# Five raw weight buffers in place of three, out of shared SBUF space, and the first half's row transposes four to five matmuls later at a stage's end

## The chip, the cores and the metric

The kernel runs on one core of a Trainium2 chip. The metric is the device time of one execution in microseconds (us); of several executions the median is given.

## What is computed

A decoder trunk of four layers on one sequence of 256 rows with 1024 features. Each layer is a SwiGLU feed-forward half step, a token mixer, and a second feed-forward half step, each between two RMS norms with a gain:

```python
def swiglu_ffn(x, w_gate_up, w_down):
    gate, up = jnp.split(x @ w_gate_up, 2, axis=-1)
    return (jax.nn.silu(gate) * up) @ w_down
...
x = x + 0.5 * rms_norm(swiglu_ffn(rms_norm(x, g0), ...), g1)     # the sandwich, in short
x = x + rms_norm(mixer(rms_norm(x, g2)), g3)
```

The hidden width is 2816. The mixer of layers 0 and 3 is a gated MLP over chunks of rows (mixer a), that of layer 1 a dilated window attention with rotary tables (mixer b), that of layer 2 a forgetting attention (mixer c). Each mixer also attends to 256 memory rows. All is in 32-bit floating point.

## The kernel before

**Stages and halves.** The 256 rows are two halves of 128, t = 0 and t = 1, held in `x[0]` and `x[1]`. The program is twelve stages: FFN(l,0), mixer, FFN(l,1) for each layer l. A stage begins with transposed inputs `xth` and `xtl` and ends with a boundary: ScalarE squares a half's result and VectorE multiplies it with the gain `gpost` (`L373`, `L374`), GpSimd makes the inverse root, VectorE adds to `x` (`L378`), ScalarE squares `x` (`L381`), GpSimd makes the second inverse root (`L348`, `L349`), VectorE writes the normed rows with the gain `gpre` (`L385`), TensorE transposes the rows (`L399`), and ScalarE and VectorE split the result into `xth` and `xtl` (`L309`, `L310`).

**Three products for one.** A 32-bit matmul is made of three faster ones: a value is split into a rounded part hi and a rest lo, and hi·hi, lo·hi and hi·lo are added up (`L334`, `L335`, `L336`; in the down projection all three are `L684`). So each unit of weights, 128x1024 numbers or 512 KB, goes this way: a transfer by SP's queue into one of RAW buffers `raw` (`L240`), ScalarE's copy into `hi` (`L309`), VectorE's subtraction into `lo` (`L310`), and then the matmuls. The pair `hi`, `lo` is a ring of ten. A `raw` buffer is free again when its `lo` is made; a ring place when the last matmul that reads it is through. The order of units is a plan; `pump` makes as many as the ring has room for, and `slot`, called after each unit's matmuls, also issues one background step (`self.bg`).

**The FFN.** The hidden columns are six sets. Sets 0, 1, 3 and 5 are plain. Sets 2 and 4 form their 2x2 blocks from seven products instead of eight (function `seven`, matmuls on `L615`); their weights are loaded into `quad` buffers (eight transfers) and VectorE adds some of them up first (`L277`). Between the products VectorE and ScalarE take results out: `L635` (function `c11`, from PSUM into `snap`), `L658` and `L659` (function `c12`). A finished set `T` is transposed on TensorE at `L557` (`turn_set`) and split into `hh` and `hl` (for the last set `eh` and `el`), the left sides of the down projection. The down projection has 22 units; the last eight are held at the end: first all eight for t = 0, then the chain of the boundary for t = 0 is issued (`turn(0)`), then the eight for t = 1, which are 48 matmuls of 128x512, then `turn(1)`. The transposes of t = 0 (`trans(0)`) are issued right after `turn(0)`, ahead of the eight units of t = 1; a scheduler that reorders by readiness then places them. The transposes of t = 1 are issued inside the next stage's first set.

**The mixers** end in the same way: `out_first` makes the out projection of t = 0, `out_rest` issues `trans(0)` and the out projection of t = 1 (`L944`; eight units, in mixer b four), then the second boundary chain.

**The scheduler.** The program is written as if in sequence; a scheduler fixes each engine's order from readiness and priority, and the engines run their lists in that order, waiting on semaphores. SP's list holds nearly all transfers.

**SBUF.** Pools hand out buffers by tag. Before the change RAW is 3; the ScalarE squares are dumped into a tag `junk`; memory rows and their chunks have the tags `gpost` and `memraw`; the two gains of a boundary have the tags `gpost` and `gpre` for the whole program and are loaded by the background step `gains` at the start of each FFN (in FFN(0,0) after set 2); the sums of the seven products have the tags `sh` and `sl`.

Of the kernel before, what the change touches and what calls it, by code (L numbers as in the profile page):

```python
# [10 lines left out]
F32 = mybir.dt.float32  # L11
# [19 lines left out]
LN_EPS = 1e-5  # L31
BIG = 1e30
RING = 10
RAW = 3
HELD = 8
GRP = 4

# [166 lines left out]
class Trunk:  # L204
# [143 lines left out]
        g.tensor_tensor(out=out, in0=ss, in1=eps_tile, op=ALU.add)  # L348
        g.tensor_tensor(out=out, in0=out, in1=self.neghalf, op=ALU.pow)  # L349

    def gain(self, l, n, tag):
        t = self.main.tile([P, D], F32, tag=tag, name=tag)
        self.nc.sync.dma_start(out=t, in_=self.io["norm_g"][l, n].partition_broadcast(P))
        return t

    def ln_stages(self, st, t, ps, post_scale, post_eps, gpost, gpre):
        nc = self.nc
        if "rows" not in st:
            st["rows"] = None
        junk = lambda: self.main.tile([P, D], BF16, tag="junk", name="junk")  # L360
        ss = self.small.tile([P, 1], F32, tag="ss", name="ss", bufs=8)
        r = self.small.tile([P, 1], F32, tag="r", name="r", bufs=8)
        ss2 = self.small.tile([P, 1], F32, tag="ss2", name="ss2", bufs=8)
        r2 = self.small.tile([P, 1], F32, tag="r2", name="r2")
        x = self.x[t]

        def rows():
            if st["rows"] is None:
                st["rows"] = self.main.tile([P, 2, D], F32, tag="rows", name="rows")
            return st["rows"][:, t, :]  # L370

        def s1():
            nc.scalar.activation(out=junk(), in_=ps, func=AF.Square, scale=post_scale, accum_out=ss)  # L373
            nc.vector.tensor_tensor(out=rows(), in0=ps, in1=gpost, op=ALU.mult)  # L374
            self.rsqrt(r, ss, post_eps)

        def s2():
            nc.vector.scalar_tensor_tensor(out=x, in0=rows(), scalar=r, in1=x, op0=ALU.mult, op1=ALU.add)  # L378

        def s3():  # L380
            nc.scalar.activation(out=junk(), in_=x, func=AF.Square, scale=1 / 32, accum_out=ss2)  # L381
            self.rsqrt(r2, ss2, self.eps1)

        def s4():
            nc.vector.scalar_tensor_tensor(out=rows(), in0=x, scalar=r2, in1=gpre, op0=ALU.mult, op1=ALU.mult)  # L385

        out = []
        if ps is not None:
            out += [s1, s2]
        if gpre is not None:  # L390
            out += [s3, s4]
        return out
# [36 lines left out]
    def setup(self):  # L429
        nc, io, c = self.nc, self.io, self.const  # L430
        self.x = [c.tile([P, D], F32, name=f"x{t}") for t in range(2)]
        self.ident = c.tile([P, P], F32, name="ident")
        nc.sync.dma_start(out=self.x[0], in_=io["x"][:P, :])
        self.gpre = self.gain(0, 0, "gpre")
# [12 lines left out]
        turn = self.boundary(None, None, self.gpre)  # L447
        turn(0)
        self.trans(0, keep=self.keep)
        turn(1)  # L450
        self.pump(most=RING)

    def setup2(self):
        nc, io, c = self.nc, self.io, self.const
        self.tri1 = c.tile([P, SEQ], F32, name="tri1")
        self.R = c.tile([P, SEQ], F32, name="R")

        def loads():
            nc.sync.dma_start(out=self.tri1, in_=io["tri1"])
            nc.sync.dma_start(out=self.mg, in_=io["mem_g"])  # L460

        def squares(t):
            m = self.main.tile([P, D], F32, tag="gpost", name="memrow")
            nc.sync.dma_start(out=m, in_=io["mem"][t * P:(t + 1) * P, :])
            ss = self.small.tile([P, 1], F32, tag="ss", name="ss", bufs=8)
            nc.scalar.activation(out=self.main.tile([P, D], BF16, tag="junk", name="junk"), in_=m, func=AF.Square,
                                 scale=1 / 32, accum_out=ss)
            self.rsqrt(self.r_mem[:, t:t + 1], ss, self.eps1)

        def inverse():  # L470
            ps = self.rot()
            for t in range(2):
                d = self.main.tile([P, SEQ], F32, tag="memraw", name="memf", bufs=2)
# [55 lines left out]
    def ffn(self, l, f, post_next, pre_next, last=False):  # L529
        nc, tc = self.nc, self.tc  # L530
        with tc.tile_pool(name=f"ffn{l}{f}", bufs=1, reuse_waits="tile") as fp:
# [61 lines left out]
            def sums():  # L593
                x11, x12, x21, x22 = (self.xf[t, h] for t in range(2) for h in range(2))
                tt = nc.vector.tensor_tensor
                out = []
                for dst, a, b, op in ((x22, x21, x22, ALU.subtract), (x21, x11, x21, ALU.subtract),
                                      (x11, x22, x11, ALU.subtract), (x12, x12, x11, ALU.add)):
                    tt(out=dst, in0=a, in1=b, op=op)
                    y = tuple(fp.tile([P, 4, P], F32R, tag=n, name=n, bufs=4) for n in ("sh", "sl"))  # L600
                    self.split(*(v.rearrange("p a b -> p (a b)") for v in y), dst)
                    out.append(y)
                S1, S3, S2, S4 = out
                a11 = tuple(v[:, 0:4, 0:P] for v in xt)
# [60 lines left out]
            gn = {"pre": None}  # L665

            def gains():
                gn["post"] = self.gain(l, post_next[0], "gpost")
                if pre_next:
                    gn["pre"] = self.gain(*pre_next, "gpre")  # L670

            if (l, f) != (0, 0):
                self.bg.append(gains)
            ys = [self.acc() for _ in range(2)]

            def hT(j, t):
                return tuple(h[:, j % 4, t * P:(t + 1) * P] for h in hs[j // 4])

            def down(j, t, w):
                a = hT(j, t)  # L680
                mm = nc.tensor.matmul
                for x, y in ((a[0], w[0]), (a[0], w[1]), (a[1], w[0])):
                    for n in range(2):
                        mm(ys[t][:, n * 512:(n + 1) * 512], x, y[:, 0, n * 512:(n + 1) * 512],  # L684
                           start=(j == 0 and x is a[0] and y is w[0]),
                           stop=(j == NF - 1 and x is a[1]))
# [14 lines left out]
            for s in range(1, SETS):  # L701
# [2 lines left out]
                    self.new_quad(fp, l, f, s + 1)  # L704
                if s in SEVEN:
                    seven(s)
                    if s == min(SEVEN) and (l, f) == (0, 0):
                        self.bg.extend(self.setup2() + [gains])
                    if s == min(SEVEN) and (l, f) == (0, 1):
                        self.bg.extend(self.rope_tables(fp))  # L710
                    if s == max(SEVEN) and f == 0:
# [22 lines left out]
                    turned(SETS - 1)  # L734
            turn = self.boundary(ys, (gn["post"], 1 / 16, self.eps16), gn["pre"])
            turn(0)
            if not last:
                self.trans(0, keep=self.keep if f else None)
            for j in range(nd, NF):
                down(j, 1, held[j - nd])  # L740
                self.slot(1)
            turn(1)
        if last:
# [1 line left out]
                nc.sync.dma_start(out=self.io["out"][t * P:(t + 1) * P, :], in_=self.x[t])  # L745

    def mem_chunk(self, k):
        m = self.main.tile([P, SEQ], F32, tag="memraw", name="memraw", bufs=2)
        self.nc.sync.dma_start(out=m, in_=self.io["mem_t"][k * P:(k + 1) * P, :])
        return m  # L750

# [180 lines left out]

        return o, [lambda j=j: self.out_step(l, o, 0, j) for j in range(n)], chain

    def out_step(self, l, o, t, j):
        if j == 0:
            o["y"].append(self.acc())
        if t == 0:
# [1 line left out]
        w = o["w"][j]  # L940
        a = tuple(v[:, j, t * P:(t + 1) * P] for v in o["yt"])
        for x, y in ((a[0], w[0]), (a[0], w[1]), (a[1], w[0])):
            for h in range(2):
                self.nc.tensor.matmul(o["y"][t][:, h * 512:(h + 1) * 512], x, y[:, 0, h * 512:(h + 1) * 512],  # L944
                                      start=(j == 0 and x is a[0] and y is w[0]),
# [1 line left out]
        self.slot(t)  # L947

    def out_rest(self, l, o):
        self.trans(0, keep=self.keep)  # L950
        for j in range(o["n"]):
            self.out_step(l, o, 1, j)
        o["turn"](1)

    def mixer(self, l, j):
# [4 lines left out]
            getattr(self, "mix_" + kind)(mp, l, j, self.xt)  # L960

    def gains(self, l):
        return self.gain(l, 3, "gpost"), self.gain(l, 4, "gpre")

    def mix_a(self, mp, l, j, xt):
        nc, io = self.nc, self.io
# [362 lines left out]
```

## Time and profile before

| | |
|---|---|
| median of 3 executions | 1900.68 us (1900.43 to 1908.29) |
| the profiled execution | 1902.04 us |
| its span (first to last instruction) | 1900.2 us |
| granted TensorE clock, mean over the span | 0.999 of full speed |
| busy: PE, PEld | 1858.8, 1550.4 us (98%, 82%) |
| busy: DVE, ACT, POOL | 1514.9, 1085.9, 59.8 us (80%, 57%, 3%) |
| moved by the DMA queues | 362.65 MB, mean 191 GB/s |

PE is TensorE's matmuls, PEld its weight loads, DVE VectorE, ACT ScalarE, POOL GpSimd, SP the engine that issues the transfers, SPq its queue. 1.84 us of the profiled execution lie outside its span. Each row of the chain and of the waits names an engine, an output tile and a line of the kernel, and what it waited for.

### The profile page before, as it was taken

To read this page: it belongs to the slowest core of one execution; us is meant where nothing else is said; L and a number is where in the kernel's file an instruction comes from. 1 tells how busy PE (TensorE), PEld (TensorE's weight loads), DVE (VectorE), ACT (ScalarE), POOL (GpSimd) and SP (SyncE) were. 2 spreads that over 40 slices of the span, in tenths; PEclk is the share of its full clock that TensorE was granted. 3 is DMA by queue.
4 is the path that set the end of the run, shared out by engine and by line. 5 is a ranking of instruction groups with operands and counts; after the bars stand their busy time and mean duration, and the time that the engine had idled before them with its cause. 6 is when DMAs were issued, how large, how long until landed. Compare 5 with 4: busy or idle time off the path is not lost.

```text
span 1900.2 us, 25015 instructions
## 1 busy us (share of the span) xinstructions
PE 1858.8 (98%) x9406; PEld 1550.4 (82%) x9406; DVE 1514.9 (80%) x1828; ACT 1085.9 (57%) x1469; POOL 59.8 (3%) x115
## 2 busy tenths in 40 slices
PE   7999999999999999999999999999999999999998
PEld 5888888787878897888888889888888878988886
DVE  6987888896879768889697966878877886878894
ACT  5655656564656545655565656555556555656562
POOL 0000100000000000000000000000000000100000
PEclk9999999999999999999999999999999999999999
DMA  8646747545663663754566357275476535747632
GB/s 295 235 167 200 233 156 266 205 140 176 233 222 115 199 203 111 266 198 145 180 231 233 112 185 238 102 246 184 151 229 227 189 127 183 243 156 244 220 105 86
DMA packets 103865, 362.65 MB, mean 191 GB/s; under 512 B 12084, under 2 KB 16576, under 8 KB 103616
## 3 DMA queue, kind: packets, MB, share of 16 engines
q1 hardware_dynamic: 103568, 359.47, 56.5%
q8 instruction: 74, 1.21, 0.3%
q0 software_dynamic: 176, 1.59, 0.2%
q14 instruction: 47, 0.39, 0.1%
HBM read 359.95 MB, written 1.06 MB: 190 GB/s over the span
## 4 chain that ended last, share of the span: by engine, by line
PE 60%; DVE 17%; DMA 12%; ACT 5%; issue 4%; POOL 1%; ACTq 0%; SPq 0%; DVEq 0%
PE acc L684 15%; DMA raw<-in_w 12%; PE rot L615 9%; PE rot L334 9%; PE rot L336 9%; PE rot L335 9%; DVE lo L310 9%; ACT hi L309 4%; DVE quad L277 3%; PE acc L944 3%; PE rot L557 1%; PE rot L399 1%; PE rot L848 1%; DVE x L378 1%; PE rot L880 1%
## 5 line engine op out<-in xcount | busy, mean ns | idle before, releaser
L310 DVE TENSOR_TENSOR lo<-raw,hi 128x1024 fp32r<-128x1024 f32 (+1 forms) x515 | 624.4, 1219 | 216.9 <-ACT hi L309 207.5
L309 ACT ACTIVATE hi<-raw 128x1024 fp32r<-128x1024 f32 (+1 forms) x515 | 542.1, 1055 | 397.0 <-DMA raw<-in_w 259.0
L334 PE MATMUL rot<-hi,xth 128*128 128x512 f32 (+3 forms) x1072 | 414.9, 387 | 2.5 <-ACT hi L309 1.6
L336 PE MATMUL rot<-hi,xtl 128*128 128x512 f32 (+3 forms) x1072 | 411.6, 384 | 1.2 <-DVE xtl L310 1.1
L335 PE MATMUL rot<-lo,xth 128*128 128x512 f32 (+3 forms) x1072 | 411.6, 384 | 0.0
L309 ACT ACTIVATE hi<-quad 128x1024 fp32r<-128x1024 f32 x224 | 232.7, 1056 | 156.5 <-DVE quad L277 83.4
L310 DVE TENSOR_TENSOR lo<-quad,hi 128x1024 fp32r<-128x1024 f32 x224 | 269.4, 1220 | 7.2 <-ACT hi L309 6.2
L334 PEld LDWEIGHTS rot<-hi,xth 128*128 128x128 f32 x1072 | 202.1, 189 | 41.4 <-ACT hi L309 2.1
L336 PEld LDWEIGHTS rot<-hi,xtl 128*128 128x128 f32 x1072 | 201.9, 188 | 41.3 <-DVE xtl L310 2.3
L335 PEld LDWEIGHTS rot<-lo,xth 128*128 128x128 f32 x1072 | 202.1, 189 | 38.2
L684 PE MATMUL acc<-lo,hh 128*128 128x512 f32 x640 | 198.9, 390 | 0.0
L684 PE MATMUL acc<-hi,hh 128*128 128x512 f32 x640 | 198.0, 390 | 0.0
L684 PE MATMUL acc<-hi,hl 128*128 128x512 f32 x640 | 197.2, 389 | 0.0
L277 DVE TENSOR_TENSOR quad<-quad 128x1024 f32<-128x1024 f32 x128 | 154.2, 1220 | 0.9
L684 PEld LDWEIGHTS acc<-hi,hl 128*128 128x128 f32 x640 | 120.1, 188 | 25.0 <-DVE hl L310 0.2
L684 PEld LDWEIGHTS acc<-lo,hh 128*128 128x128 f32 x640 | 120.2, 188 | 24.8
L684 PEld LDWEIGHTS acc<-hi,hh 128*128 128x128 f32 x640 | 119.5, 188 | 24.3
L615 PE MATMUL rot<-hi,sh 128*128 128x512 f32 x256 | 103.0, 402 | 6.8 <-DVE snap L635 6.8
L615 PE MATMUL rot<-lo,sh 128*128 128x512 f32 x256 | 100.0, 391 | 0.0
L615 PE MATMUL rot<-hi,sl 128*128 128x512 f32 x256 | 97.4, 390 | 0.0
L374 DVE TENSOR_TENSOR rows<-acc,gpost 128x1024 f32<-128x1024 f32 x24 | 29.3, 1222 | 74.9 <-ACT junk L373 74.8
L615 PE MATMUL rot<-hi,xtl 128*128 128x512 f32 x192 | 74.8, 389 | 0.0
(212 smaller groups left out, 2439.8 us busy)
## 6 DMA issues: line engine op xcount, KB each, us to landing
raw<-in_w SPq DMA_DIRECT2D x504, 512.0 KB, 4.3
quad<-in_w SPq DMA_DIRECT2D x128, 512.0 KB, 5.8
gpre<-in_norm_g SPq DMA_DIRECT2D x12, 512.0 KB, 5.1
gpost<-in_norm_g SPq DMA_DIRECT2D x12, 512.0 KB, 5.4
memraw<-in_mem_t SPq DMA_DIRECT2D x32, 128.0 KB, 3.2
raw<-in_w SPq DMA_DIRECT2D x8, 384.0 KB, 3.5
sw<-in_sw SPq DMA_DIRECT2D x2, 768.0 KB, 8.1
cb<-cd POOLq DMA_DIRECT2D x1, 1536.0 KB, 9.9
```

What stands on the lines that cost most here:

```text
L277: add = lambda x, y: self.nc.vector.tensor_tensor(out=x, in0=x, in1=y, op=ALU.add)
L309: self.nc.scalar.activation(out=hi, in_=src, func=AF.Copy)
L310: self.nc.vector.tensor_tensor(out=lo, in0=src, in1=hi.bitcast(F32), op=ALU.subtract)
L334: mm(out, a[0], b[0], start=start, stop=False)
L335: mm(out, a[0], b[1], start=False, stop=False)
L336: mm(out, a[1], b[0], start=False, stop=stop)
L374: nc.vector.tensor_tensor(out=rows(), in0=ps, in1=gpost, op=ALU.mult)
L378: nc.vector.scalar_tensor_tensor(out=x, in0=rows(), scalar=r, in1=x, op0=ALU.mult, op1=ALU.add)
L399: nc.tensor.transpose(ps[:, (k - k0) * P:(k - k0 + 1) * P], rows[:, k * P:(k + 1) * P], self.ident)
L615: nc.tensor.matmul(ps, a[i], w[j][:, kk, :], start=fresh and h == kk == i == j == 0, stop=h == kk == i == 1, skip_group_check=True)
L684: mm(ys[t][:, n * 512:(n + 1) * 512], x, y[:, 0, n * 512:(n + 1) * 512], start=(j == 0 and x is a[0] and y is w[0]), stop=(j == NF - 1 and ...
L944: self.nc.tensor.matmul(o["y"][t][:, h * 512:(h + 1) * 512], x, y[:, 0, h * 512:(h + 1) * 512], start=(j == 0 and x is a[0] and y is w[0]) ...
```

## The change

- RAW becomes 5.
- To make room: the dump of the squares, the memory chunks `memraw` and the tiles `memf` share the tag `snap` (four buffers); the memory rows use the tag `rows`; the sums of the seven products become one tile with the tag `S`, and the FFN's two gains are buffers of the same tag `S`. A mixer's two gains are buffers of the mixer's own pool. The first gain of the program sits in the tag `mgh`.
- Since `S` is shared with the sums, the FFN's `gains` step is put on the background list after set 4 (the last with seven products) and no longer at the FFN's start; so is the work on the memory rows in FFN(0,0) (`setup2`).
- `trans(0)` is issued inside the down projection of t = 1: in the last unit but one, after the first two of its six matmuls. In `out_rest` the same, if there are eight units; with four (mixer b) it stays in front.

```diff
-RAW = 3
+RAW = 5
...
+    def dump(self):
+        return self.main.tile([P, D], BF16, tag="snap", name="junk", bufs=4)
+
+    def gain(self, l, n, t):
         self.nc.sync.dma_start(out=t, in_=self.io["norm_g"][l, n].partition_broadcast(P))
         return t
...
-                    y = tuple(fp.tile([P, 4, P], F32R, tag=n, name=n, bufs=4) for n in ("sh", "sl"))
+                    y = fp.tile([P, 2, 4, P], F32R, tag="S", name="sums", bufs=4)
+                    y = (y[:, 0], y[:, 1])
...
             def gains():
-                gn["post"] = self.gain(l, post_next[0], "gpost")
+                tile = lambda n: fp.tile([P, D], F32, tag="S", name=n, bufs=4)
+                gn["post"] = self.gain(l, post_next[0], tile("gpost"))
                 if pre_next:
-                    gn["pre"] = self.gain(*pre_next, "gpre")
-
-            if (l, f) != (0, 0):
-                self.bg.append(gains)
+                    gn["pre"] = self.gain(*pre_next, tile("gpre"))
...
-            def down(j, t, w):
+            def down(j, t, w, mid=None):
                 a = hT(j, t)
                 mm = nc.tensor.matmul
                 for x, y in ((a[0], w[0]), (a[0], w[1]), (a[1], w[0])):
+                    if mid and y is w[1]:
+                        mid()
                     for n in range(2):
...
-                    if s == min(SEVEN) and (l, f) == (0, 0):
-                        self.bg.extend(self.setup2() + [gains])
+                    if s == max(SEVEN):
+                        self.bg.append(gains)
+                    if s == max(SEVEN) and (l, f) == (0, 0):
+                        self.bg.extend(self.setup2())
...
             turn(0)
-            if not last:
-                self.trans(0, keep=self.keep if f else None)
             for j in range(nd, NF):
-                down(j, 1, held[j - nd])
+                late = j == NF - 2 and not last
+                down(j, 1, held[j - nd], (lambda: self.trans(0, keep=self.keep if f else None)) if late else None)
                 self.slot(1)
             turn(1)
...
     def out_rest(self, l, o):
-        self.trans(0, keep=self.keep)
+        trans = lambda: self.trans(0, keep=self.keep)
+        late = o["n"] - 2 if o["n"] == 8 else 0
+        if not late:
+            trans()
         for j in range(o["n"]):
-            self.out_step(l, o, 1, j)
+            self.out_step(l, o, 1, j, trans if late and j == late else None)
         o["turn"](1)
```

The multiset of instructions of TensorE, GpSimd and the transfers is the same; ScalarE gets two more loads of its function tables (seven for five), around the rotary tables. What moves is the order. TensorE's list at the end of FFN(0,1), which leads into FFN(1,0); `eh` and `el` are the last set's columns, so the rows at the foot are the last two units, before the change:

```order
L684 MATMUL acc<-hi,hh 128x512 x2
L684 MATMUL acc<-lo,hh 128x512
L399 MATMUL rot<-ident,rows 128x128 x8
L684 MATMUL acc<-lo,hh 128x512
L684 MATMUL acc<-hi,hl 128x512 x2
L684 MATMUL acc<-hi,eh 128x512 x2
L684 MATMUL acc<-lo,eh 128x512 x2
L684 MATMUL acc<-hi,el 128x512 x2
L684 MATMUL acc<-hi,eh 128x512 x2
L684 MATMUL acc<-lo,eh 128x512 x2
L684 MATMUL acc<-hi,el 128x512 x2
L334 MATMUL rot<-hi,xth 128x512
```

The same place on TensorE after the change:

```order
L691 MATMUL acc<-lo,hh 128x512 x2
L691 MATMUL acc<-hi,hl 128x512 x2
L691 MATMUL acc<-hi,eh 128x512 x2
L400 MATMUL rot<-ident,rows 128x128 x8
L691 MATMUL acc<-lo,eh 128x512 x2
L691 MATMUL acc<-hi,el 128x512 x2
L691 MATMUL acc<-hi,eh 128x512 x2
L691 MATMUL acc<-lo,eh 128x512 x2
L691 MATMUL acc<-hi,el 128x512 x2
L334 MATMUL rot<-hi,xth 128x512
```

Of the 48 matmuls of t = 1, 33 stood ahead of the transposes and 15 behind; now 38 stand ahead and 10 behind. The ends of the other FFNs and of both mixers a read the same way; at mixer c it is seven matmuls, and mixer b is as it was.

VectorE's list at the same place before the change, from the rows of t = 0 to the rows of t = 1 (`x_72` is `x[0]`, `x_73` is `x[1]`):

```order
L385 SCALAR_TENSOR_TENSOR rows<-x_72,r_4067,gpre 128x1024
L310 TENSOR_TENSOR lo<-raw,hi 128x1024
L310 TENSOR_TENSOR xtl<-rot,xth 128x4x128 x2
L310 TENSOR_TENSOR lo<-raw,hi 128x1024 x3
L374 TENSOR_TENSOR rows<-acc,gpost 128x1024
L378 SCALAR_TENSOR_TENSOR x_73<-rows,r,x_73 128x1024
L310 TENSOR_TENSOR lo<-raw,hi 128x1024
L385 SCALAR_TENSOR_TENSOR rows<-x_73,r_4199,gpre 128x1024
```

The same place on VectorE after the change:

```order
L386 SCALAR_TENSOR_TENSOR rows<-x_72,r_4062,gpre 128x1024
L310 TENSOR_TENSOR lo<-raw,hi 128x1024 x3
L310 TENSOR_TENSOR xtl<-rot,xth 128x4x128 x2
L310 TENSOR_TENSOR lo<-raw,hi 128x1024 x2
L375 TENSOR_TENSOR rows<-acc,gpost 128x1024
L310 TENSOR_TENSOR lo<-raw,hi 128x1024
L379 SCALAR_TENSOR_TENSOR x_73<-rows,r,x_73 128x1024
L386 SCALAR_TENSOR_TENSOR rows<-x_73,r_4194,gpre 128x1024
```

Two more `lo` stand ahead of `xtl`, and one that stood ahead of the second `rows` stands ahead of the update of `x[1]`, behind which the second half's chain goes on.

The third place is VectorE in set 2 of FFN(0,1), ahead of `c11`'s addition (`L635`, after the change `L641`). The rotary tables (`rt`, made once for mixer b) were computed in mixer a of layer 0 and FFN(0,1)'s first set. Before the change:

```order
L277 TENSOR_TENSOR quad<-quad 128x1024
L310 TENSOR_TENSOR lo<-raw,hi 128x1024
L277 TENSOR_TENSOR quad<-quad 128x1024
L310 TENSOR_TENSOR lo<-raw,hi 128x1024
L310 TENSOR_TENSOR lo<-quad,hi 128x1024 x2
L310 TENSOR_TENSOR lo<-raw,hi 128x1024
L635 TENSOR_TENSOR snap<-snap,rot 128x512
```

The same place after the change:

```order
L310 TENSOR_TENSOR lo<-raw,hi 128x1024
L520 SCALAR_TENSOR_TENSOR rt<-rt 128x64
L310 TENSOR_TENSOR lo<-quad,hi 128x1024
L525 TENSOR_SCALAR rt<-rt 128x64
L515 TENSOR_SCALAR rt<-rt 128x64
L526 TENSOR_SCALAR rt<-rt 128x64
L517 TENSOR_SCALAR rt<-rt 128x64
L518 TENSOR_SCALAR rt<-rt 128x64
L310 TENSOR_TENSOR lo<-quad,hi 128x1024
L310 TENSOR_TENSOR lo<-raw,hi 128x1024
L641 TENSOR_TENSOR snap<-snap,rot 128x512
```

Of the rotary tables' 29 small operations, 22 now stand in sets 1 and 2 ahead of that addition, and the other 7 behind it.

More of the change, by code (lines that the diff above doesn't have):

```diff
@@ L349, in rsqrt @@
         g.tensor_tensor(out=out, in0=out, in1=self.neghalf, op=ALU.pow)
-    def gain(self, l, n, tag):
-        t = self.main.tile([P, D], F32, tag=tag, name=tag)
+    def dump(self):
+        return self.main.tile([P, D], BF16, tag="snap", name="junk", bufs=4)
+    def gain(self, l, n, t):
         self.nc.sync.dma_start(out=t, in_=self.io["norm_g"][l, n].partition_broadcast(P))
@@ L359, in ln_stages @@
             st["rows"] = None
-        junk = lambda: self.main.tile([P, D], BF16, tag="junk", name="junk")
         ss = self.small.tile([P, 1], F32, tag="ss", name="ss", bufs=8)
@@ L372, in s1 @@
         def s1():
-            nc.scalar.activation(out=junk(), in_=ps, func=AF.Square, scale=post_scale, accum_out=ss)
+            nc.scalar.activation(out=self.dump(), in_=ps, func=AF.Square, scale=post_scale, accum_out=ss)
             nc.vector.tensor_tensor(out=rows(), in0=ps, in1=gpost, op=ALU.mult)
@@ L380, in s3 @@
         def s3():
-            nc.scalar.activation(out=junk(), in_=x, func=AF.Square, scale=1 / 32, accum_out=ss2)
+            nc.scalar.activation(out=self.dump(), in_=x, func=AF.Square, scale=1 / 32, accum_out=ss2)
             self.rsqrt(r2, ss2, self.eps1)
@@ L433, in setup @@
         nc.sync.dma_start(out=self.x[0], in_=io["x"][:P, :])
-        self.gpre = self.gain(0, 0, "gpre")
+        self.gpre = self.gain(0, 0, self.main.tile([P, 2, D], F32, tag="mgh", name="gpre")[:, 0, :])
         nc.sync.dma_start(out=self.ident, in_=io["ident"])
@@ L456, in setup2 @@
         self.R = c.tile([P, SEQ], F32, name="R")
+        both = []
         def loads():
@@ L462, in squares @@
         def squares(t):
-            m = self.main.tile([P, D], F32, tag="gpost", name="memrow")
+            if t == 0:
+                both.append(self.main.tile([P, 2, D], F32, tag="rows", name="memrow"))
+            m = both[0][:, t, :]
             nc.sync.dma_start(out=m, in_=io["mem"][t * P:(t + 1) * P, :])
             ss = self.small.tile([P, 1], F32, tag="ss", name="ss", bufs=8)
-            nc.scalar.activation(out=self.main.tile([P, D], BF16, tag="junk", name="junk"), in_=m, func=AF.Square,
+            nc.scalar.activation(out=self.dump(), in_=m, func=AF.Square,
                                  scale=1 / 32, accum_out=ss)
@@ L472, in inverse @@
             for t in range(2):
-                d = self.main.tile([P, SEQ], F32, tag="memraw", name="memf", bufs=2)
+                d = self.main.tile([P, SEQ], F32, tag="snap", name="memf", bufs=4)
                 nc.vector.tensor_scalar(out=d[:, :P], in0=self.ident, scalar1=self.r_mem[:, t:t + 1], scalar2=None,
@@ L747, in mem_chunk @@
     def mem_chunk(self, k):
-        m = self.main.tile([P, SEQ], F32, tag="memraw", name="memraw", bufs=2)
+        m = self.main.tile([P, SEQ], F32, tag="snap", name="memraw", bufs=4)
         self.nc.sync.dma_start(out=m, in_=self.io["mem_t"][k * P:(k + 1) * P, :])
@@ L933, in out_first, with out_step @@
         return o, [lambda j=j: self.out_step(l, o, 0, j) for j in range(n)], chain
-    def out_step(self, l, o, t, j):
+    def out_step(self, l, o, t, j, mid=None):
         if j == 0:
@@ L942, in out_step @@
         for x, y in ((a[0], w[0]), (a[0], w[1]), (a[1], w[0])):
+            if mid and y is w[1]:
+                mid()
             for h in range(2):
@@ L962, in gains @@
     def gains(self, l):
-        return self.gain(l, 3, "gpost"), self.gain(l, 4, "gpre")
+        return tuple(self.gain(l, n, self.mp.tile([P, D], F32, name=f"g{n}")) for n in (3, 4))
     def mix_a(self, mp, l, j, xt):
```

## The prediction

> **What bounds the kernel now.** The page comes first, then the waits of TensorE: which engine has no slack, and what its stops are.
>
> ```profile
> span 1900.2 us, 25015 instructions
> PE 1858.8 (98%) x9406; PEld 1550.4 (82%) x9406; DVE 1514.9 (80%) x1828; ACT 1085.9 (57%) x1469; POOL 59.8 (3%) x115
> ```
>
> TensorE is busy 98% of the span; VectorE at 80% is the next. The change removes no matmul, so it can gain only where TensorE stops. The view of its waits (us in total, times, longest) names nearly all of them:
>
> ```profile
> PE rot L399 <- DVE rows L385: 15.5, 11, 8.4
> PE rot L615 <- DVE snap L635: 6.8, 7, 1.8
> PE rot L557 <- DVE T L659: 4.8, 6, 1.5
> PE rot L557 <- DVE T L719: 2.1, 5, 0.7
> PE rot L334 <- ACT hi L309: 1.6, 1, 1.6
> PE rot L336 <- DVE xtl L310: 1.1, 1, 1.1
> ```
>
> These are 31.9 us. The 8.4 is the program's first transpose and stays. A stop costs more than its idle time, because matmuls overlap:
>
> ```profile
> 473.09 0.62 PE L684 MATMUL acc<-hi,eh 128*128 128x512 f32 x2
> 474.45 0.39 PE L334 MATMUL rot<-hi,xth 128*128 128x512 f32 x1
> ```
>
> Two matmuls take 0.62, one 0.39, so the pitch is 0.23 and each stop hides another 0.39 − 0.23 = 0.16. With that the ten L399 stops cost 15.5 − 8.4 + 1.6 = 8.7, the seven L615 stops 6.8 + 1.1 = 7.9, the eleven L557 stops 4.8 + 2.1 + 1.8 = 8.7. With the two at the start that is about 28 us, 1.5% of the time; the change is aimed at these.
>
> What stands behind the L615 and L557 stops? Each is preceded by a run of VectorE without a gap. At the longest, the timeline and the windows (PE, PEld, DVE, ACT, POOL busy; clock, DMA share, GB/s) show it:
>
> ```profile
> 324.22 1.06 ACT L309 ACTIVATE hi<-raw 128x1024 fp32r<-128x1024 f32 x1 [1.68 <-DMA raw<-in_w]
> 325.31 1.22 DVE L310 TENSOR_TENSOR lo<-raw,hi 128x1024 fp32r<-128x1024 f32 x1 [1.52 <-ACT hi L309]
> 352.69 0.68 DVE L635 TENSOR_TENSOR snap<-snap,rot 128x512 f32<-128x512 f32 x1
> 353.43 0.50 PE L615 MATMUL rot<-hi,sh 128*128 128x512 f32 x1 [1.76 <-DVE snap L635]
> ```
>
> ```profile
> 300.00:325.00 25.00, 25.00 (x115) 20.77 (x116) 19.33 (x24) 16.04 (x20) 0.00 (x0) 1.00 0.90 297
> 325.00:353.00 28.00, 26.66 (x122) 21.85 (x120) 27.69 (x27) 16.89 (x20) 0.00 (x0) 1.00 0.28 85
> ```
>
> Up to 325 VectorE idles 5.67 of 25 us, waiting for ScalarE, which waits for a `raw` transfer. From 325 to 353 it works 27.69 of 28 and comes 1.76 late. So the cause lies in front: weights that landed earlier would have let it start its work earlier. An L557 stop has the same look:
>
> ```profile
> 565.72 1.06 ACT L309 ACTIVATE hi<-raw 128x1024 fp32r<-128x1024 f32 x1 [1.32 <-DMA raw<-in_w]
> 567.96 0.69 DVE L659 TENSOR_TENSOR T<-T,snap 128x512 f32<-128x512 f32 x1
> 568.70 0.98 PE L557 MATMUL rot<-ident,T 128*128 128x128 f32 x7 [1.47 <-DVE T L659]
> ```
>
> That three `raw` buffers are what holds the transfers back is in the waits of the other two engines and in the transfer's own time:
>
> ```profile
> ACT hi L309 <- DMA raw<-in_w: 259.0, 226, 3.7
> SPq L240 <- DVE lo L310: 1260.3, 510, 22.7
> raw<-in_w SPq DMA_DIRECT2D x504, 512.0 KB, 4.3
> ```
>
> SP waits 510 times for a `lo`, that is for a buffer. A buffer's round is 4.3 landing + 1.06 hi + 1.22 lo = 6.6 us, so three give a unit each 2.2 us at best, five each 1.3, near VectorE's 1.22.
>
> **The change, part by part.** The sum is made against the profiled execution, 1902.04 us, which is 1.36 above the median.
>
> *Transposes of t = 0.* The boundary into FFN(1,0):
>
> ```profile
> 468.68 1.28 DVE L385 SCALAR_TENSOR_TENSOR rows<-x,r,gpre 128x1024 f32<-128x1024 f32 x1 [0.71 <-POOL r L349]
> 470.11 1.07 PE L399 MATMUL rot<-ident,rows 128*128 128x128 f32 x8 [0.74 <-DVE rows L385]
> 471.41 1.29 DVE L310 TENSOR_TENSOR xtl<-rot,xth 128x512 fp32r<-128x512 f32 x2 [0.31 <-ACT xth L309]
> 482.45 1.28 DVE L385 SCALAR_TENSOR_TENSOR rows<-x,r,gpre 128x1024 f32<-128x1024 f32 x1 [1.04 <-POOL r L349]
> 483.98 1.03 PE L399 MATMUL rot<-ident,rows 128*128 128x128 f32 x8
> ```
>
> The stop is 0.74 + 0.16 = 0.90. Five more matmuls ahead, 5 × 0.23 = 1.15, cover it. The next stage starts 0.9 earlier. Now the second half: its rows end at 482.45 + 1.28 = 483.73, and TensorE reaches their transposes at 483.98, 0.25 later. The rows come from a chain of ScalarE, VectorE and GpSimd steps behind the last matmul of t = 1; it starts 0.9 earlier, but the new order puts one `lo`, 1.22, ahead of the update of `x[1]` in it. I take it as ending where it did. Then TensorE, 0.9 early, waits at the second transposes and **gives the 0.9 back**. Into a mixer the distance is larger:
>
> ```profile
> 210.56 1.28 DVE L385 SCALAR_TENSOR_TENSOR rows<-x,r,gpre 128x1024 f32<-128x1024 f32 x1 [0.71 <-POOL r L349]
> 216.35 0.38 PE L399 MATMUL rot<-ident,rows 128*128 128x128 f32 x2
> ```
>
> 216.35 − 211.84 = 4.5 us: nothing is given back. So the four ends that lead into a mixer keep 4 × 0.9 = **3.6**, the six others (three FFN ends, mixers a, c, a) nothing; bounds for these six: 0 to 5.1 gained (8.7 − 3.6).
>
> *xtl behind two more `lo`.* `xtl` is needed by the next stage's third matmul. It was begun at 471.41; two more `lo` are 2.44, so its first half (0.65) ends at 474.5 at worst, and the third matmul comes at 474.45 − 0.9 + 2 × 0.23 = 474.0. VectorE idled 0.31 there and the first `lo` ran inside the old wait, so I put the cost at nothing; bounds 0 to 0.5 on ten ends, 5.
>
> *The start.* Two stops there:
>
> ```profile
> 11.58 1.28 DVE L385 SCALAR_TENSOR_TENSOR rows<-x,r,gpre 128x1024 f32<-128x1024 f32 x1 [1.08 <-POOL r L349]
> 13.52 0.79 PE L336 MATMUL rot<-hi,xtl 128*128 128x512 f32 x1 [1.12 <-DVE xtl L310]
> 22.48 0.50 PE L334 MATMUL rot<-hi,xth 128*128 128x512 f32 x1 [1.63 <-ACT hi L309]
> ```
>
> In the new order the second `rows` stand behind `xtl`, and five units are under way instead of three, so the fifth need not wait: 1.12 + 1.63 = **2.7**, bounds 1 (only the smaller goes) and 4.
>
> *Five raws at the L557 and L615 stops.* A unit each 1.3 us instead of 2.2 lets VectorE work ahead in its 5.67 idle us, three times the longest stop. What then limits it is the ring of ten, which the change leaves; so a fifth of these stops I let stand: L557 8.7 × 0.8 = **7.0**; L615 (7.9 − 1.9) × 0.8 = **4.8**. Bounds 0 and 8.7 + 7.9.
>
> *The stop at 353.* I take it out of the L615 sum, since the rotary tables now stand ahead of it:
>
> ```profile
> L515 DVE SCALAR_TENSOR_TENSOR rt<-rt x12: 217/226/227, 274.5 to 298.8; 128x64 f32<-128x64 f32 x12
> 295.55 1.28 ACT L522 ACT_TABLE_LOAD   x1
> 296.84 0.26 ACT L522 ACTIVATE cos<-rt 128x64 f32<-128x64 f32 x1
> ```
>
> 22 × 0.226 = 5.0 us, against the 5.67 idle that opens up: about even, so its 1.9 stay. Bounds 0 and 1.9 + 5.0. The two more table loads are 2 × 1.28 on ScalarE, 57% busy, with other work to cover them: nothing. [...]
>
> *Gains.* 24 transfers of 512 KB, the same number, later in the stage, when set 4 is through; nothing waits for them before the boundary. Zero.
>
> Sum: 3.6 + 2.7 + 7.0 + 4.8 = **18.1**. The profiled execution becomes 1902.0 − 18.1 = 1883.9, the median 1900.7 − 18.1 = **1882.6 us**.
>
> **The rivals.** *B, the transfers are near their limit.* Between 300 and 325 the queues are busy 0.90 of the time at 297 GB/s: more of them in flight could bring at most 297 / 0.90 = 330, a tenth more. If that holds ahead of most stops, five buffers only wait longer; start and mixers stay, 6.3 saved, 1894.4 us. Against it: 0.28 at 325 to 353 and 191 GB/s over the span; transfers have room as soon as they may begin sooner. [...] Chance 0.18.
>
> *C, nothing is given back.* With raws in hand the second half's chain runs ahead too, and the remains of the stops go: 18.1 + 5.1 (six ends) + 1.7 + 1.2 + 1.9 = 28.0, so 1872.7 us. For it: the chain's steps wait for ScalarE work that waits for raws. Against it: the 0.25 us of distance, and one more `lo` in the chain. Chance 0.14.
>
> *D, slower: xtl waits for a raw.* VectorE works in order, and the extra `lo` ahead of `xtl` each need a landed unit. If at a stage's end the last of them is still under way, VectorE stands, with `xtl` behind it, and TensorE at its third matmul: up to one landing, 4.3 us, at ten ends, 43. It decides from 18.1 / 10 = 1.8 us an end; at 4.3 the time is 1900.7 − 18.1 + 43 = 1925.6 us. Against it: at a stage's end units are held for 48 matmuls, and raws fill meanwhile. Chance 0.05.
>
> *E, the transposes still wait*: the rows of t = 0 come as much later as the transposes do. Then 3.6 is lost: 14.5 saved, 1886.2 us. Chance 0.05.
>
> **How the numbers follow.** The forecast has 0.58, B 0.18, C 0.14, D and E 0.05 each. The range reaches from C with the start's upper end (1872.7 − 1.3 = 1871) to B (1895); D lies outside, and some of the forecast's unknown tails. A measurement of this kernel can tell about 0.5%, 9.5 us, from no change: below 1891.2 is faster. Forecast, C and E are (0.77, less 0.02 for the forecast's poor end, plus 0.03 of B, where the limit holds only in part): faster 0.78; B's rest and that end: same 0.17; D: slower 0.05.
>
> **What would show it.** ScalarE's wait for `raw` (259.0) falls by more than half, SP's for `lo` stays; L557 and L615 leave the head of TensorE's waits, the one near 353 stays. L399 stops of t = 0 vanish at ten ends, and stops at the second transposes appear in front of six stages. The forecast is wrong if ScalarE's wait for `raw` stays near 259 (B), if no L399 stop appears (C), or if L336 waits for `xtl` (D).

## The result and the profile after

The changed kernel takes 1877.68 us (median of 4 executions, 1876.93 to 1881.52), the kernel before 1902.38 beside it: a ratio of 0.9869, 95% interval 0.9842 to 0.9896. That is 24.7 us less, where 18.1 were forecast; the time lies in the stated range. The first half's transposes moved by five matmuls at nine stage ends and by seven at mixer c's, so the title's "four to five" is a little low. The profiled execution went from a span of 1900.2 to one of 1875.1, 25.1 us less. The page after the change:

```profile
span 1875.1 us, 25124 instructions
PE 1855.1 (99%) x9406; PEld 1550.2 (83%) x9406; DVE 1517.5 (81%) x1828; ACT 1092.6 (58%) x1471; POOL 67.7 (4%) x115
```

TensorE's busy time fell by 3.7 us only; the rest is idle time that is gone. Its waits in the changed kernel (us in total, times, longest):

```profile
PE rot L400 <- DVE rows L386: 10.3, 5, 8.2
PE rot L400 <- DVE rt L510: 0.5, 1, 0.5
PE rot L334 <- ACT hi L309: 0.5, 1, 0.5
PE rot L856 <- DVE p L910: 0.4, 1, 0.4
PE rot L335 <- DVE lo L310: 0.3, 1, 0.3
PE rot L336 <- DVE xtl L310: 0.3, 1, 0.3
```

No row of L562 (L557 before) or L621 (L615 before) is left in it: all eighteen stops are gone in this execution, the one at 353 us too. Of L400, 8.2 are the first transposes of the program; the other 2.1 and the row of 0.5 are five stops at the second half's transposes, which did not exist before. This list holds only gaps over 0.15 us between matmuls. The waits of the weight loads (PEld) show two places where a matmul still comes a little late:

```profile
PEld rot L621 <- DVE snap L641: 4.8, 15, 0.5
PEld rot L336 <- DVE xtl L310: 4.0, 10, 0.7
```

The wait that stood behind it all, ScalarE's for a raw transfer, was 259.0 us in 226 places and is now

```profile
ACT hi L309 <- DMA raw<-in_w: 34.6, 52, 2.1
```

The boundary into FFN(1,0) again, TensorE and the steps it depends on, from the timeline of the changed kernel:

```profile
457.90 1.28 DVE L386 SCALAR_TENSOR_TENSOR rows<-x,r,gpre 128x1024 f32<-128x1024 f32 x1 [0.71 <-POOL r L349]
459.10 3.49 DVE L310 TENSOR_TENSOR lo<-raw,hi 128x1024 fp32r<-128x1024 f32 x3
459.57 1.03 PE L400 MATMUL rot<-ident,rows 128*128 128x128 f32 x8
462.51 1.28 DVE L310 TENSOR_TENSOR xtl<-rot,xth 128x512 fp32r<-128x512 f32 x2
463.25 0.19 PEld L336 LDWEIGHTS rot<-hi,xtl 128*128 128x128 f32 x1 [0.33 <-DVE xtl L310]
463.25 0.50 PE L336 MATMUL rot<-hi,xtl 128*128 128x512 f32 x1
473.13 0.41 PE L400 MATMUL rot<-ident,rows 128*128 128x128 f32 x2 [0.51 <-DVE rows L386]
```

The first transposes begin without a stop. `xtl` starts behind three `lo` without a gap; its first half ends near 463.2, and the weights that are made of it load 0.33 late. Matmuls start 0.23 apart as a rule; the one on `xtl` starts 0.30 behind the one before it, and the next 0.34 behind that, so 0.18 is lost. At 473.13 the second half's transposes stop TensorE for 0.51, with the overlap 0.67 of the 0.90 that was saved.

The stretch ahead of the old stop at 353 us, with the same columns as in the prediction (PE, PEld, DVE, ACT, POOL; clock, DMA share, GB/s); 25 us before the run of VectorE, and the run up to its end:

```profile
293.00:318.00 25.00, 25.00 (x116) 20.76 (x115) 23.53 (x29) 17.98 (x23) 0.00 (x0) 1.00 0.89 317
318.00:345.20 27.20, 27.12 (x125) 22.23 (x123) 26.89 (x45) 14.36 (x16) 0.00 (x0) 1.00 0.25 88
```

VectorE's idle time ahead of the run is 1.47 us where it was 5.67; into what opened up went the rotary tables, and the addition at L641 ends early enough that TensorE loses 0.24 there where it lost 1.9.

### The profile page after: what moved, and what is told of

Same layout as the page of the kernel before. It is cut to its first block, busy times and chain, and to the rows that moved or that the text cites. A ratio compares the mean times of both kernels' runs of the same rounds, so it can differ in the third digit from the quotient of the medians.

```text
span 1875.1 us, 25124 instructions
## 1 busy us (share of the span) xinstructions
PE 1855.1 (99%) x9406; PEld 1550.2 (83%) x9406; DVE 1517.5 (81%) x1828; ACT 1092.6 (58%) x1471; POOL 67.7 (4%) x115
## 4 chain that ended last, share of the span: by engine, by line
PE 88%; DVE 6%; issue 3%; ACT 1%; POOL 1%; DMA 1%; SPq 0%; ACTq 0%; DVEq 0%; POOLq 0%
PE acc L691 22%; PE rot L621 16%; PE rot L334 13%; PE rot L336 13%; PE rot L335 13%; PE acc L954 3%; DVE lo L310 3%; PE rot L562 2%; PE rot L856 1%; PE acc L874 1%; DMA raw<-in_w 1%; PE rot L888 1%; DVE x L379 1%; PE rot L400 1%; DVE rows L375 1%
## 5 line engine op out<-in xcount | busy, mean ns | idle before, releaser
L309 ACT ACTIVATE hi<-raw 128x1024 fp32r<-128x1024 f32 (+1 forms) x515 | 536.2, 1053 | 266.5 <-PE acc L691 84.1
L334 PE MATMUL rot<-hi,xth 128*128 128x512 f32 (+3 forms) x1072 | 415.2, 387 | 0.5 <-ACT hi L309 0.5
L336 PE MATMUL rot<-hi,xtl 128*128 128x512 f32 (+3 forms) x1072 | 412.2, 385 | 0.4 <-DVE xtl L310 0.3
L336 PEld LDWEIGHTS rot<-hi,xtl 128*128 128x128 f32 x1072 | 201.7, 188 | 42.7 <-DVE xtl L310 4.0
L334 PEld LDWEIGHTS rot<-hi,xth 128*128 128x128 f32 x1072 | 201.8, 188 | 39.1 <-ACT hi L309 1.1
L621 PE MATMUL rot<-hi,sums 128*128 128x512 f32 x512 | 169.0, 396 | 0.1
L691 PEld LDWEIGHTS acc<-lo,hh 128*128 128x128 f32 x640 | 120.1, 188 | 25.1
L621 PEld LDWEIGHTS rot<-hi,sums 128*128 128x128 f32 x512 | 96.1, 188 | 24.3 <-DVE snap L641 4.8
L621 PE MATMUL rot<-lo,sums 128*128 128x512 f32 x256 | 99.8, 390 | 0.0
L348 POOL TENSOR_TENSOR r<-ss,thin 128x1 f32<-128x1 f32 x48 | 23.5, 490 | 1577.5 <-ACT junk L374 1484.7
L621 PE MATMUL rot<-hi,xtl 128*128 128x512 f32 x192 | 74.8, 389 | 0.0
```

The costliest lines, as they stand in the source:

```text
L309: self.nc.scalar.activation(out=hi, in_=src, func=AF.Copy)
L334: mm(out, a[0], b[0], start=start, stop=False)
L336: mm(out, a[1], b[0], start=False, stop=stop)
L621: nc.tensor.matmul(ps, a[i], w[j][:, kk, :], start=fresh and h == kk == i == j == 0, stop=h == kk == i == 1, skip_group_check=True)
```

## The experiments

The theory to begin with had two parts that add up: five buffers remove the waits for raw transfers, and the later transposes remove the stops at the boundaries. Its rivals: that the moved loads did it and not the number of buffers, and that the transposes' place matters through the order of other work. All medians stand beside runs of the kernel before on the same chip, 1902.8 to 1903.9 us.

**Three buffers, all else changed.**

```diff
-RAW = 5
+RAW = 3
```

> The changed kernel with three raw buffers again, all else as changed. Theory 1 (the number of buffers): the L557 and L615 stops, 8.7 + 7.9 us before, come back, so about 17 us over the changed kernel's 1877.7: 1893 to 1897, and ScalarE's wait for raw is near 250 us again (34.6 after the change). Theory 2 (the gains and the other loads that were moved out of the crowded stretch made room, not the buffers): at most 1882, ScalarE's wait for raw stays under 100.

Measured: 1922.04 us, ratio 1.0095 (1.0074 to 1.0117). ScalarE's wait for raw is back at 276.0 us in 224 places, so the number of buffers it was. But the kernel is 19 us slower than before the change, which neither theory had: something in the rest of the change costs a great deal, and five buffers hide it.

**Transposes at the old place, five buffers.**

```diff
             turn(0)
+            if not last:
+                self.trans(0, keep=self.keep if f else None)
             for j in range(nd, NF):
-                late = j == NF - 2 and not last
+                late = False
```

and the same in `out_rest`.

> The changed kernel with the first half's transposes issued at their old place, five buffers kept. Theory 1 (two independent gains): the ten L400 stops at the stages' ends come back with 0.9 us each, less the 5 x 0.67 us that were given back at the second transposes and less the 0.7 us of two late xtl: about 8.7 - 3.4 - 0.7 = 4.6 slower, 1882. Rival (with five buffers the rows come early enough by themselves): no difference, 1877 to 1879, no L400 stops at the ends.

Measured: 1880.31, ratio 0.9878 (0.9859 to 0.9896), 2.6 above the changed kernel, where 4.6 were expected; the two intervals overlap. The ten stops are back in its waits, with five raws in hand as well:

```profile
PE rot L400 <- DVE rows L386: 15.2, 11, 8.1
PE rot L562 <- DVE T L728: 1.6, 3, 0.6
PEld rot L336 <- DVE xtl L310: 0.3, 1, 0.3
```

The last row is what the expectation had too small: 4.0 us of late `xtl` in the changed kernel, nearly none here. Counted by the starts of the matmuls, the late `xtl` costs the changed kernel 0.17 to 0.57 at nine of the ten ends, 2.3 us, and not 0.7 at two. So the ten stops of 8.7, less 3.5 given back at the second transposes, less 2.3, leave 2.8, close to the measured 2.6.

**Four buffers, all else changed** (`RAW = 4`).

> The changed kernel with four raw buffers. A buffer's round of 6.6 us gives a unit each 1.65 us. Theory 1: three quarters or more of the buffers' gain is there already, 1878 to 1882, ScalarE's wait for raw between 50 and 130. Were the fifth buffer what counts, the time would be near 1890.

Measured: 1898.43, ratio 0.9971 (0.9958 to 0.9984), a miss by 16 us: the fifth buffer is worth 20.7, more than all the L557 and L615 stops together. The waits show that it isn't those stops:

```profile
PE rot L400 <- DVE rows L386: 17.6, 6, 8.1
PE acc L874 <- ACT qm L840: 4.7, 2, 3.0
PE rot L621 <- DVE snap L641: 3.7, 2, 3.5
PE rot L400 <- DVE rt L510: 2.3, 1, 2.3
```

L562 is absent, as with five. What is new are long stops at the second transposes (the two L400 rows, less the 8.1 of the program's start), in mixer a (`qm`) and one of 3.5 in the first set with seven products (L621). All its stops together are 17.5 us more than those of the changed kernel, and TensorE's granted clock was lower: 0.50 from 81.70 to 84.00, behind the stop of 3.5 us, 0.57 from 1661.30 to 1665.00, behind one of 3.0 for `qm`, and 0.996 over the span where the changed kernel's is 0.999. By these two averages it costs another 0.003 × 1899.7 = 5.7, an estimate: 23.2 of the 24.6 us between the two spans.

**The later transposes alone**, in the kernel before, three buffers: the edit of `down`, `out_step` and `out_rest` in the change's diff, nothing else.

> The kernel before with nothing but the later transposes; three buffers, the gains at their old place. Theory 1: the stops at four ends into mixers go (3.7 us), at the six others most is given back (0 to 1.5 kept): 1897 to 1899. Rival (the transposes' place also frees the L557 and L615 stops, since the order of lo changes with it): 1890 or less.

Measured: 1914.08, ratio 1.0059 (1.0039 to 1.0079): slower than before by 11 us. The idea of two gains that add up falls. At the end of layer 0's mixer a, ScalarE, VectorE and TensorE of this kernel:

```profile
298.22 1.06 ACT L309 ACTIVATE hi<-raw 128x1024 fp32r<-128x1024 f32 x1 [1.52 <-DMA raw<-in_w]
299.32 1.22 DVE L310 TENSOR_TENSOR lo<-raw,hi 128x1024 fp32r<-128x1024 f32 x1 [1.36 <-ACT hi L309]
300.46 1.28 DVE L378 SCALAR_TENSOR_TENSOR x<-rows,r,x 128x1024 f32<-128x1024 f32 x1
303.95 1.28 DVE L385 SCALAR_TENSOR_TENSOR rows<-x,r,gpre 128x1024 f32<-128x1024 f32 x1 [0.51 <-POOL r L349]
305.38 0.41 PE L399 MATMUL rot<-ident,rows 128*128 128x128 f32 x2 [3.06 <-DVE rows L385]
```

The `lo` that the new order puts ahead of the update of `x[1]` (L378) waits 1.36 us for its hi, hi waits for a raw transfer, and the chain behind it ends so late that TensorE stops for 3.06 us. This is the mechanism of the prediction's rival D, only that what comes late is the second half's rows and not `xtl`. It isn't the whole of the 11 us: stops for rows rose by 4.2 (from 15.5 to 19.7), while two stops for `qm` in mixer a, 4.0 together, are new, the L557 and L615 stops fell by 4.2, and the granted clock was 0.50 from 245.80 to 249.20, behind one of the `qm` stops, and 0.997 over the span where the kernel before has 0.999, by estimate 0.002 × 1910.9 = 3.8 us. Why `qm` is late here wasn't traced. The third theory: the later transposes cost where raws are short and gain where they are in hand.

**Four and three buffers, transposes at the old place** (the edits above, with `RAW = 4` and `RAW = 3`).

> The changed kernel with four raw buffers and the first half's transposes at their old place. Theory 3 (the later transposes bring one more lo into the second half's chain, which waits for a raw transfer unless buffers enough are in hand; so the shift costs with three or four buffers and gains with five): the 17.6 us of waits for rows of the four-buffer kernel fall to about 15, ten short stops, the stops of 2 us or more at the second transposes go, the clock drops behind long stops too: 1881 to 1887. Rival (a fourth buffer is simply too little, wherever the transposes stand): 1895 or more.

> The changed kernel with three raw buffers and the first half's transposes at their old place: what is left of the change is the sharing of space and the later gains, memory rows and rotary tables. Theory 3: the second transposes' stops of 2 us go, so clearly below the 1922 of the same kernel with the later transposes: 1903 to 1911. Rival (the moved loads are what made that kernel slow): 1915 or more.

Measured: 1894.34, ratio 0.9950 (0.9932 to 0.9969), and 1920.20, ratio 1.0079 (1.0052 to 1.0106). With four buffers the early place is 4 us better (1898.4), with five 2.6 us worse, which is the sign change of the third theory, though the intervals overlap in both pairs; with three the places are 1.8 apart, which tells nothing. But neither time is in its range. With three buffers, and transposes where they always were, the shared space and the loads moved with it cost 16 us against the kernel before: the rival held there. The largest single place is mixer a; VectorE, ScalarE and TensorE of the three-buffer kernel:

```profile
224.69 2.92 DVE L1026 TENSOR_SCALAR bt<-bt 128x768 f32<-128x768 f32 x1 [1.50 <-DMA bt<-in_sb]
...
228.64 0.94 ACT L1010 ACTIVATE vr<-vr,vr__2115 128x768 f32<-128x768 f32 x1 [6.93 <-DVE vr L1008]
...
245.12 1.06 ACT L309 ACTIVATE hi<-raw 128x1024 fp32r<-128x1024 f32 x1 [1.99 <-DMA raw<-in_w]
...
247.44 0.58 ACT L842 ACTIVATE qm<-rot 128x512 f32<-128x512 f32 x1
248.07 0.80 PE L876 MATMUL acc<-km,qm 64*128 64x256 f32 x2 [4.76 <-ACT qm L842]
```

The mixer's own loads are issued later than before, `bt` lands late, VectorE waits for it, ScalarE stands 6.93 us behind VectorE, no raw buffer is freed meanwhile, and when the work goes on the three raws are used up and each hi waits for a landing, with `qm` behind them in ScalarE's order. The changed kernel has the first half of this too:

```profile
217.03 0.94 ACT L1008 ACTIVATE vr<-vr,vr__2119 128x768 f32<-128x768 f32 x1 [5.13 <-DVE vr L1006]
```

but there `qm` stops nobody: five raws bridge it. The wait behind VectorE came with the layout: 4.6 to 7.7 us there with three, four and five buffers, at most 1.7 where the loads weren't moved. The two `qm` stops, 8.1, and the clock behind the one above, 0.50 from 248.00 to 252.00, 2.0 us by estimate, are 10 of the 23.5 us by which the span exceeds that of the kernel before; over the whole span the clock was 0.992 where it was 0.999. Why the other sets with seven products are later in the three-buffer kernel too (9.3 us of L621 waits in five places, before 6.8 in seven) wasn't traced.

**A fourth buffer alone**, in the kernel before; the dumps, the memory chunks and `memf` share `snap` to make the room, gains, tables and transposes stay. The main lines:

```diff
-RAW = 3
+RAW = 4
...
-        junk = lambda: self.main.tile([P, D], BF16, tag="junk", name="junk")
+        junk = lambda: self.main.tile([P, D], BF16, tag="snap", name="junk", bufs=4)
...
-        m = self.main.tile([P, SEQ], F32, tag="memraw", name="memraw", bufs=2)
+        m = self.main.tile([P, SEQ], F32, tag="snap", name="memraw", bufs=4)
```

> The kernel before with a fourth raw buffer and nothing else but the room for it (the dumps of the squares and the memory chunks share the snap buffers); gains, rotary tables and transposes at their old places. Theory 3: most of the L557 and L615 stops go, the ten L399 stops stay: 1884 to 1890. Rival (the moved gains are needed as well): 1895 or more.

Measured: 1891.11, ratio 0.9926 (0.9901 to 0.9951), a little above the range expected. One buffer with nothing moved brings half of the change's gain; with the loads moved it is 1894.34, 3.2 worse, though the intervals overlap. ScalarE's wait for raw:

```profile
ACT hi L309 <- DMA raw<-in_w: 93.4, 107, 2.5
```

The fifth buffer alone was not run: its room is the space that the gains gave up.

**The second half's transposes three matmuls later.**

```diff
-                        pair(held[4 + i], u, i, t)
+                        late = t == 0 and i == 3
+                        pair(held[4 + i], u, i, t, (lambda: self.trans(1, keep=self.keep)) if late else None)
                         self.slot(t)
-                        if t == 0 and i == 2:
-                            self.trans(1, keep=self.keep)
```

where `pair` calls the last argument between its two halves.

> The changed kernel with the second half's transposes three matmuls later in the next FFN's first set. If the five stops of 0.67 us there only come from rows that end late, 3 x 0.23 = 0.68 us of matmuls cover them: 3.4 less, 1874.3. Rival (xth and xtl of the second half are then late by as much for the matmuls right behind): no difference, 1877 to 1879, with stops at L334 or L336 in their place.

Measured: 1877.69, ratio 0.9852 (0.9826 to 0.9879). The stops are gone, the time is not: 

```profile
PE rot L400 <- DVE rows L386: 8.3, 1, 8.3
PE rot L564 <- DVE T L729: 1.7, 3, 0.7
PE rot L857 <- DVE p L911: 1.4, 2, 1.0
```

Hardly a stop at L334 or L336 took their place (0.4 and 0.3), so that rival's mechanism fell, though the time is the one it named. The other two rows are no answer: the changed kernel's second trace, in the next experiment, has such stops in the same places (2.6 and 1.7) without this edit. They come and go between executions of one kernel, so 3.4 us of stops cannot be followed into the median here, and whether the edit gains stays open.

**The changed kernel, the early place, and the later place only at the four ends into a mixer**, once more on one chip. The last is `late = j == NF - 2 and not last and f == 0`, with `trans(0)` in front otherwise and in `out_rest`.

> The changed kernel itself, beside the three below on one chip: 1876 to 1880.

> Five buffers with the transposes at their old place, once more. By the stops (ten of 0.9 come back, five of 0.67 go) it should be 3 to 5 us above the changed kernel; were the shift worth nothing with five buffers, within 1 us of it.

> The changed kernel with the later transposes only at the four ends that lead into a mixer; the six ends into an FFN as before the change. If the give-back at the second transposes is nearly whole there (0.67 of 0.5 to 0.97), those six ends bring 4.9 - 3.4 = 1.5 us, and this kernel is 0 to 2 us above the changed one; if they brought all they remove, 5 above.

Measured: 1878.63 (0.9862, 0.9839 to 0.9885), 1881.21 (0.9876, 0.9855 to 0.9896) and 1880.00 (0.9872, 0.9852 to 0.9893). The order of the three is as expected, with 2.6 and 1.4 above the changed kernel, but each difference is within its interval. The stops themselves can be counted in the traces and are those expected; the spans of the three traces (1879.7, 1880.7, 1878.2) are not in that order. The changed kernel's second trace has L562 stops that the first had not:

```profile
PE rot L400 <- DVE rows L386: 10.3, 5, 8.3
PE rot L562 <- DVE T L728: 2.6, 4, 1.2
```

Its span was 1879.7 against 1875.1: a few us of the gain vary from one execution to the next.

**More VectorE work ahead of the addition at L641.** In `c11`, twice a maximum of a tile with itself:

```diff
+                    for _ in range(2):
+                        tt(out=v["P1"], in0=v["P1"], in1=v["P1"], op=ALU.max)
                     tt(out=v["P1"], in0=v["P1"], in1=b, op=ALU.add)
```

> The changed kernel with two more additions' worth of VectorE work (2 x 0.68 us, a maximum of a tile with itself, which changes nothing) ahead of the first addition of each of the 16 sets with seven products. Theory (with five buffers VectorE's run through these sets has just caught up: the weight loads behind that addition wait 0.3 us at 15 of 16 places): 16 x 1.36 = 22 us of work, of which at least a third shows as stops at L621: 7 to 20 us slower. Rival (VectorE, 81% busy, now has room there): less than 2 us.

Measured: 1882.89, ratio 0.9886 (0.9866 to 0.9906), 4.3 above the changed kernel beside it. Neither expectation: VectorE's busy time rose by 16.0 us, not by the 22 of the expectation, and 4 show. No stop at L621 is in the waits of TensorE's matmuls, but the weight loads behind the addition (now L643) wait longer:

```profile
PEld rot L621 <- DVE snap L643: 8.4, 16, 0.6
```

The changed kernel beside it has 4.8 in 15 places there, as in its first trace. The 3.6 more are close to the 4.3 by which the time rose. So in these sets TensorE's weight loads still wait for the addition, about 0.3 us each without this edit, but three quarters of the extra work went into time that VectorE had free.

## Why the prediction was right, step by step

*The bound and its cause* (TensorE's stops; raw transfers behind the L557 and L615 stops): shown. Three, four and five buffers in the changed layout with the early transposes gave 1920.2, 1894.3 and 1880.3 us.

*L557 and L615, 7.0 + 4.8 forecast.* They brought 8.7 + 7.9, the whole, in the first trace; in the second, four L562 stops of 2.6 us are there. The step that was off is "a fifth of these stops I let stand" together with "its 1.9 stay" for the stop at 353. The size of the rotary work was nearly right (4.5 for 5.0), and so was the idle time that it went into (5.67 down to 1.47). The stop went all the same: the addition begins 64.1 us behind the stage's first matmul where it began 65.2 behind it, and TensorE itself loses 0.7 at the second transposes on the way. The two more table loads show no cost beyond their own 1.28: the one at 345.43 begins 0.02 behind the activation before it, and the next activation begins 0.01 behind its end. The last run shows that VectorE had room for most of 16 us more in these sets. Whether the ring of ten, put forward as the next bound, limits anything no run tested.

*`xtl` behind two more `lo`, put at nothing*: this term was mis-sized. `xtl` is late at nine of ten ends, by 0.17 to 0.38 at eight and 0.57 at one, 2.3 us together. The prediction had worked out 0.5 at worst and set it aside because VectorE idled 0.31 there; the rows of the boundary above show the `lo` running through without a gap.

*Transposes into mixers, 3.6 forecast*: 3.7 of stops went, and 1.3 of the late `xtl` fell here: 2.4.

*Transposes into FFNs, nothing forecast*: 4.9 went, 3.5 was given back (0.67 or 0.68 at five ends, 0.12 at mixer c's), 1.0 of the late `xtl` fell here: 0.4 kept. The give-back is shown, and its step, that the chain would end where it had, was right to 0.06 us at five ends of the six.

*The start, 2.7 forecast*: TensorE is busy 16.05 of the first 25 us where it was 13.04, 3.0.

Together 3.0 + 2.4 + 0.4 + 8.7 + 7.9 = 22.4; the span fell by 25.1, and the other 2.7 are not assigned.

*Rival B*: excluded, ScalarE's wait for raw fell by seven eighths. Its "at most 330 GB/s" was wrong besides: in the stretch above the queues moved 317 at a share of 0.89, which by the same division would allow 356, and the kernel before itself moved 385 from 353.4 to 357.0. *Rival C*: nearer to the result than the forecast in the stops, wrong in the give-back. *Rival D*: absent with five buffers; its sign, L336 waiting for `xtl`, is there (0.3 in the waits, 4.0 in the weight loads), but without its cause: the late `xtl` stands behind `lo` that run without a gap, not behind a transfer. With three it is part of what made the later transposes cost 11 us. Whether it comes is a matter of how many raws are in hand, and the change raised that number. *Rival E*: excluded, the first transposes stop nowhere.

What the prediction did not see is that the parts don't add up. Making room for the buffers cost 16 us where there were three of them, and the later transposes cost 11 with three buffers in the old layout, 4 with four in the new. The 40 us that two more buffers brought in the new layout paid for it. The forecast counted neither cost; it held since with five buffers both vanish. The result exceeds it by 6.6, and 4.8 of that are the stops that it had let stand. That five were enough was luck: the same reckoning by the round of a buffer gave 1878 to 1882 for four, and four took 1898.

## What to carry to other kernels

Count a prefetch buffer by the longest stretch in which nothing frees one, not by its mean round: here the mean round said that four would nearly do (6.6 / 4 = 1.65 us a unit), while stalls of 5 to 7 us in one mixer emptied four and not five. When a move puts one more piece of prefetch work into an in-order chain, ask what that piece waits for; the same move gained 2.6 us with five buffers and lost 11 with three in the kernel before. And test a change's parts at the old setting too: a part may only be free because another covers it.

## What the runs showed of the hardware

After some stops TensorE's granted clock fell to 0.50. The four-buffer kernel at its longest stop after the start (a wait of 3.51 us, ending at 81.69), and the three-buffer kernel after one of 5.79, ending at 246.30, both with the later transposes, columns as above:

```profile
77.00:81.60 4.60, 1.18 (x6) 0.63 (x4) 4.60 (x6) 3.27 (x5) 0.00 (x0) 0.98 0.96 296
81.70:84.00 2.30, 2.30 (x6) 1.82 (x7) 2.30 (x4) 0.61 (x1) 0.00 (x0) 0.50 1.01 411
```

```profile
246.30:250.30 4.00, 4.00 (x17) 3.17 (x18) 3.86 (x5) 3.31 (x4) 0.00 (x0) 0.50 0.77 235
250.30:253.00 2.70, 2.70 (x16) 2.70 (x15) 2.63 (x8) 1.58 (x8) 0.00 (x0) 0.58 0.86 228
```

So the stop of 5.8 us costs, by estimate, another 4 × 0.50 + 2.7 × 0.42 = 3.1 us. The length of a stop alone doesn't decide. In the kernel with the later transposes alone, behind a wait of 1.98 us ending at 244.5 the clock was 0.50 (from 245.80 to 249.20), and behind the one of 3.06 us ending at 305.4 it was 1.00 (to 310.60):

```profile
242.40:245.80 3.40, 1.42 (x11) 0.97 (x11) 2.92 (x5) 2.02 (x3) 1.25 (x1) 1.00 0.81 275
245.80:249.20 3.40, 3.40 (x18) 3.40 (x18) 2.79 (x4) 2.92 (x6) 0.00 (x0) 0.50 0.64 188
300.40:303.80 3.40, 1.91 (x9) 1.26 (x7) 3.01 (x7) 3.01 (x5) 0.66 (x2) 1.00 0.72 246
303.80:307.20 3.40, 1.82 (x12) 1.69 (x13) 3.08 (x9) 2.31 (x4) 0.11 (x1) 1.00 0.84 312
307.20:310.60 3.40, 3.40 (x16) 2.75 (x15) 3.39 (x8) 2.56 (x5) 0.00 (x0) 1.00 0.67 181
```

What decides it no run tested. The first fence also shows the queues at 411 GB/s for 2.3 us, well over what the prediction took for their limit from 297 at a share of 0.90.

One short VectorE operation, begun during a GpSimd one over a large tile, ended only behind it. The scaling of `bt` took 0.55 us in the kernel before, where it began after GpSimd's 3.53 us masking of `sw` had ended; in the changed kernel it began during it:

```profile
211.01 4.58 POOL L1023 TENSOR_TENSOR sw<-sw,tri 128x1536 f32<-128x1536 f32 x1 [6.63 <-DMA bt<-in_sb]
```

```profile
213.33 2.68 DVE L1024 TENSOR_SCALAR bt<-bt 128x768 f32<-128x768 f32 x1
```

It took 2.68 us and ended 216.01 − 215.59 = 0.4 us after GpSimd's. In the three-buffer kernel with the transposes at their old place it took 2.92, shown above, while GpSimd's masking ran from 223.69 to 227.19, and 2.51 in layer 3's mixer; there too it began during the masking, and ended 0.4 behind it. In seven other places (the kernel before, the later transposes alone and four buffers with the early ones, both layers each, and layer 3 of the changed kernel) it began after the masking had ended and took 0.54 to 0.55. Not every VectorE operation stands so: the two halves of `xtl` at 212.13, during the masking shown, took their usual 1.28. No run tested by itself what makes the difference.
